# A hybrid S5/HGRN2 block: a hand-ordered front, S5 column work on GpSimd, and S5 input products stacked in 96 rows

## The chip, the cores and the metric

The kernel runs on one core of a Trainium2 chip. The metric is device time in microseconds of one execution; times are the median of several runs, and the profile is one further execution. The engines are TensorE (PE in the profile, with its weight loads as PEld), VectorE (DVE), ScalarE (ACT), GpSimd (POOL) and SyncE (SP, which only issues DMAs). Every engine works through its own instructions in order; semaphores tie the engines together.

## The reference

One decoder block on x of 256 tokens by 2048 channels in fp32, cut to what matters here:

```python
h = _rmsnorm(x, ln_mix_g[l])
proj = h @ w_in[l]                                # 2048 x 9216
u_s5, q_h, f_h, i_h, g_h, gate_s5, gate_hgrn = jnp.split(proj, _in_splits(), axis=-1)
y_s5 = _s5_branch(u_s5, ...) @ w_proj_s5[l]
y_hgrn = _hgrn2_branch(q_h, f_h, i_h, g_h, ...) @ w_proj_hgrn[l]
merged = jax.nn.sigmoid(gate_s5) * y_s5 + jax.nn.sigmoid(gate_hgrn) * y_hgrn
x = x + merged @ w_out[l]
x = x + _conv_glu_ffn(_rmsnorm(x, ln_ffn_g[l]), w_up[l], conv_w[l], conv_b[l], w_down[l])
return _rmsnorm(x, ln_final_g)

# inside _s5_branch: 64 groups of 16 channels, 64 states each
dt = jnp.exp(log_dt)[:, None]
mag = jnp.exp(lam_re * dt)
abar_re, abar_im = mag * jnp.cos(lam_im * dt), mag * jnp.sin(lam_im * dt)
coef_re, coef_im = ...                            # (abar - 1) / lambda, complex
bu_re = jnp.einsum('blgc,gpc->blgp', uf, b_re)    # and bu_im with b_im
bb_re, bb_im = ...                                # coef * bu, complex
...                                               # s[t] = abar * s[t-1] + bb[t]
y = einsum(s_re, c_re) - einsum(s_im, c_im) + d * uf
z = jax.nn.gelu(y)
z = z * jax.nn.sigmoid(z @ w_glu + b_glu)
```

## The kernel before

All large products run as **steps**. A step is 512 KB of weights (`[128, 1024]` fp32): `load_step` issues its load on SP's queue (tag `wr`, four buffers, issued LOAD_AHEAD = 5 steps ahead), `split_step` makes a high part `wh` (a cast on ACT, L256) and a low part `wl` (a subtraction on VectorE), two steps ahead (LA = 2, three buffers each), and TensorE adds up high x high, high x low and low x high. In `fm_job` (channels on partitions) a step is 8 matmuls of 512 columns on `wh` and 8 of 256 on `wl`; in `tm_job` (tokens on partitions) it is 12 of 512. There are 480 steps, executed in the order of their creation: 144 over w_in (u 16, q 16, g 16, f 16, the gates 64, v 16), 8 over w_glu, 16 and 16 over the two projections, 32 over w_out, 176 over w_up, 88 over w_down. Nearly every operation of VectorE and TensorE goes through the helper `Metered`, so these carry its line, L106, in the profile; tiles tell them apart.

**The front.** x (four chunks of 512 channels, 512 KB each) is loaded on SP between the first weights. `x_chunk(g)` transposes a chunk on TensorE into `ax` (PSUM), scales it by `g_mix` into the high part of `hT` on ACT (L405) and the low part on VectorE. `x_first` makes `g_mix` from `packG`, handles chunk 0 and puts dummy matmuls (`warm_up`) behind. The four u jobs come one after the other, four steps each (one for each chunk), so steps 0 to 3 need all four chunks; chunks 1 to 3 are transposed in the middle of steps 0 to 2 (`st.between`). `x_norm` (after step 2) adds the squares of x on VectorE and makes the row scale `r_x`, spread to `R_x` for the epilogues.

**Two side jobs** are Python generators. `side_run`, after every step, lets the current one advance while the planner's sum of VectorE costs is below that of TensorE, with at most two pauses (`yield`) a step for S5 and three for HGRN2; a yielded value means to wait until that job is finished. S5 comes first and must be done before the w_glu steps (index 144); HGRN2 follows and must be done at index 168. The rest of the order is left to the framework's compile-time scheduler, apart from places tied by `issue_after`.

`side_s5` loads b and c on ACT's queue (L585, L587), transposes parameters packed in rows (`packB`, `packC`) into columns, and then does about 130 small operations of 128x32 on VectorE: the HGRN2 lower bound, dt, the decay `mag_c`, the angle reduced in three parts (`hi`, `lo`), two sines on ACT (L663, L664), the input coefficients `cr` and `ci`. It builds tables of angles (`tabA`, `tabB`; summed for each ct on GpSimd by `angle_sum`, L741), the scaled b (`BB`) and the transposed c (`CT`). Then it loops over ct = 0 to 7 (128 channels each, two pairs). `b_trans(ct)` transposes two 128x128 blocks of b (`zmat`) and splits b and u into high and low parts in one tile; `b_proj(ct, pair)` multiplies them into the PSUM tile `bu`, twelve matmuls of 32 rows (3 parts, 2 components, 2 halves). VectorE rotates the result, runs four scans, rotates back, and TensorE applies c (`output`).

Parameters in rows come by small DMAs: eight on POOL's queue, four on SP's (`load_params`, behind the fifth weight load).

Of the kernel before, what the change touches and what calls it, by code (L numbers as in the profile page):

```python
# [17 lines left out]
P = 128  # L18
# [76 lines left out]
class Metered:  # L95
# [5 lines left out]
    def __getattr__(self, name):  # L101
        fn = getattr(self._e, name)

        def call(*args, **kw):
            self._load[self._key] += self._cost(name, args, kw)
            return fn(*args, **kw)  # L106
        return call
# [3 lines left out]
def kernel(  # L111
# [28 lines left out]
    WARM_H = 6  # L140
    NORM_AT = 2
# [35 lines left out]
    ones = cst.tile([P, P], F32, name="ones")  # L177
    G.memset(ones, 1.0)
# [7 lines left out]
    S.dma_start(out=cf, in_=cst_f)  # L186
    ident = cf[:, C_ID:C_ID + P]

    x_tok = [[unit() for _ in range(2)] for _ in range(2)]
# [8 lines left out]
    S.dma_start(out=packG, in_=rows(ln_mix_g))  # L198
    G.memset(packA, 0.0)
    ldt = pack[0:64, 5 * P:5 * P + 2]  # L200

    def load_params():
        S.dma_start(out=packA[16:32, :], in_=rows(lb_logits))
        S.dma_start(out=packA[56:72, :], in_=rows(ln_ffn_g))
        S.dma_start(out=packA[72:104, :], in_=a_re.rearrange("o (q g) p -> (o q) (g p)", g=2))
        S.dma_start(out=packB[0:32, :], in_=a_im.rearrange("o (q g) p -> (o q) (g p)", g=2))

# [8 lines left out]
    G.dma_start(out=packC[2][8:96, :], in_=rows(conv_b))  # L216
    masks = cst.tile([P, 5, 16], U8, name="masks")
# [22 lines left out]
    def weight_step(src, mm, need=None, extra_load=None):  # L240
        st = Step()
        st.src, st.mm, st.need, st.extra_load = src, mm, need, extra_load
        st.after = st.between = None
        steps.append(st)
        return st

    def load_step(st):
        uid[0] += 1
        st.w = wp.tile([P, 1024], F32, tag="wr", name=f"wr{uid[0]}", bufs=4)
        S.dma_start(out=v3(st.w, st.src.shape[1]), in_=st.src)  # L250

    def split_step(st):
# [3 lines left out]
        A.copy(st.wh, st.w)  # L256
# [14 lines left out]
    def fm_job(wap, c0, nkc, xs, epi, need=None, extra_load=None, wide=False):  # L271
# [5 lines left out]
        for g in range(ng):  # L277
            def mm(st, g=g):
                if g == 0:
                    box["ps"] = mm_bank()  # L280
                ps = box["ps"]
                wh, wl = v3(st.wh, 4), v3(st.wl, 4)
                for part in range(2):
                    if part == 1 and st.between is not None:
                        st.between()
# [107 lines left out]
    def x_chunk(g, between=None):  # L393

        for h in range(2):
            if h == 1 and between is not None:
                between()
# [5 lines left out]
            for a in range(2):  # L403
                kc = 4 * g + 2 * h + a
                A.activation(out=hT[:, kc, 0, :], in_=ax[:, a * T:(a + 1) * T], func=AF.Copy, scale=g_mix[:, kc:kc + 1])  # L405
# [5 lines left out]
        box["x"] = [getattr(i, "ins", i) for i in (last, lastp)]  # L411

    @contextmanager
    def behind_x():

        with tc.issue_after(box["x"][0]), tc.issue_after(box["x"][1]):
            yield

    def x_first():
        ax = axbank()  # L420
        PE.transpose(ax[:, 0:16], packG, ident[:16, :16])
        V.tensor_copy(g_mix, ax[:, 0:16])
        x_chunk(0, lambda: split_step(steps[0]))
        with behind_x():
            warm_up(WARM_H, ones)

    def x_norm():
        ss = cst.tile([P, 2, 4], F32, name="ss_x")
        for g in range(4):
            for j in range(2):  # L430
                xc = x_tok[j][g // 2][:, (g % 2) * 512:(g % 2) * 512 + 512]
                junk = tmp()
                V.scalar_tensor_tensor(out=junk, in0=xc, scalar=1.0, in1=xc, op0=ALU.mult, op1=ALU.mult,
                                       accum_out=ss[:, j, g:g + 1])
# [3 lines left out]
        broadcast_rows(R_x, r_x)  # L438
# [92 lines left out]
    u_jobs = [fm_job(w_in, 256 * p, 16, xs_hw, epi_u(p), wide=True) for p in range(4)]  # L531
# [25 lines left out]

    def exp_parts(new, xin):
# [18 lines left out]
        V.tensor_scalar(out=si, in0=n, scalar1=127.0, scalar2=8388608.0, op0=ALU.add, op1=ALU.mult)
        return e, si.bitcast(F32)

    def side_s5():  # L580

        bn, cn = unit(), unit()
        bn_r, bn_i = bn[:, 0:512], bn[:, 512:1024]
        for dst, src in ((bn_r, b_re), (bn_i, b_im)):
            A.dma_start(out=v3(dst, 32), in_=src.rearrange("o (q g) p c -> (o g p) q c", g=2))  # L585
        for dst, src in ((cn[:, 0:512], c_re), (cn[:, 512:1024], c_im)):
            A.dma_start(out=v3(dst, 8), in_=src.rearrange("o (t g) c p -> (o g c) t p", g=8))  # L587
# [14 lines left out]

        l0, l1 = colA[:, 16:24], colA[:, 24:32]
        m, e0, e1 = new()[:, 0:8], new()[:, 0:8], new()[:, 0:8]
        V.tensor_tensor(out=m, in0=l0, in1=l1, op=ALU.max)
        z = new()[:, 0:16]
        V.tensor_tensor(out=z[:, 0:8], in0=l0, in1=m, op=ALU.subtract)
        V.tensor_tensor(out=z[:, 8:16], in0=l1, in1=m, op=ALU.subtract)
        e, s = exp_parts(new, z)
        V.scalar_tensor_tensor(out=z, in0=e, scalar=1.0, in1=s, op0=ALU.add, op1=ALU.mult)  # L610
        V.tensor_tensor(out=e0, in0=z[:, 0:8], in1=z[:, 8:16], op=ALU.add)
        V.reciprocal(out=e1, in_=e0)
        V.tensor_tensor(out=lb_col, in0=z[:, 0:8], in1=e1, op=ALU.mult)
        V.tensor_scalar(out=oml_col, in0=lb_col, scalar1=-1.0, scalar2=1.0, op0=ALU.mult, op1=ALU.add)
        yield

        new = sp_tiles()
        lam_im = colB[:, 0:32]
        lam_re, dt_, la, th, mag, em1 = (new() for _ in range(6))
        V.tensor_scalar(out=lam_re, in0=colA[:, 72:104], scalar1=S5_MAX_RE, scalar2=None, op0=ALU.min)  # L620
        e, s = exp_parts(new, colB[:, 32:64])
        V.scalar_tensor_tensor(out=dt_, in0=e, scalar=1.0, in1=s, op0=ALU.add, op1=ALU.mult)
# [781 lines left out]
```

## Time and profile before

| | us |
|---|---|
| median of 3 runs | 1422.99 (1422.62 to 1424.28) |
| the profiled execution's own time | 1422.75 |
| its span | 1420.6 |
| TensorE busy | 1403.4 (99%) |
| VectorE busy | 1056.9 (74%) |
| ScalarE busy | 757.7 (53%) |
| GpSimd busy | 38.0 (3%) |
| read from HBM, written | 266.73 MB, 10.49 MB |

A row of the instruction view has start, length, engine, line, operation, tile written <- tiles read, shapes and how many are merged, then in brackets the idle time before it and what ended that. In groups the numbers after the bar are busy time in us and the mean in ns, then idle time before. The name `u` covers all the 4 KB work tiles, `t` the 2 KB ones, `d` scratch in DRAM. Ends of matmuls are modelled, so starts are the safer numbers for TensorE.

### The profile page before, as it was taken

The numbers are of one execution on the slowest core, as the hardware profiler recorded it, in microseconds if no ns is written. First come the engines' busy times: TensorE is split into PE (matmuls) and PEld (weight loads), VectorE is DVE, ScalarE is ACT, GpSimd is POOL, SyncE is SP. The second block draws the span as 40 slices with busy tenths as digits, with TensorE's granted clock in tenths as the row PEclk, the third lists the DMA queues.
The fourth block names the chain that finished last, engine by engine and source line by source line (L and its number), as shares of the span: only waits on it lengthen the run. The fifth ranks groups of instructions, "written<-read, shape, count | busy, mean of one in ns | idle before, by whom it ended". The sixth has DMA issues, their size and how long they took to land.

```text
span 1420.6 us, 20722 instructions
## 1 busy us (share of the span) xinstructions
PE 1403.4 (99%) x8008; PEld 1182.1 (83%) x8008; DVE 1056.9 (74%) x1453; ACT 757.7 (53%) x962; POOL 38.0 (3%) x33
## 2 busy tenths in 40 slices
PE   9999999999999999999999999999999999999997
PEld 7878887877778787888888888888888888888885
DVE  7999989998978968655777777777777775545454
ACT  5455576665655464454555555555555554434343
POOL 1040000000001000000000000000000000000000
PEclk9999999999999999999999999999999999999999
DMA  7865767666767466666666666666666666666653
GB/s 237 219 195 149 218 206 219 202 205 187 210 191 262 154 199 207 220 212 207 193 191 185 188 192 187 186 191 191 185 189 191 188 187 193 201 193 201 194 194 125
DMA packets 215940, 278.58 MB, mean 196 GB/s; under 512 B 19938, under 2 KB 141042, under 8 KB 215841
## 3 DMA queue, kind: packets, MB, share of 16 engines
q1 hardware_dynamic: 198496, 266.57, 60.5%
q10 hardware_dynamic: 17088, 10.49, 2.4%
q8 instruction: 63, 1.03, 0.3%
q14 instruction: 37, 0.30, 0.1%
q0 software_dynamic: 256, 0.19, 0.0%
HBM read 266.73 MB, written 10.49 MB: 195 GB/s over the span
## 4 chain that ended last, share of the span: by engine, by line
PE 95%; DVE 2%; DMA 1%; ACT 1%; issue 0%; POOL 0%; ACTq 0%; DVEq 0%; POOLq 0%
PE mm L106 87%; PE ax L106 7%; DVE u L106 1%; PE bu L106 1%; DMA u<-d 1%; DVE wl L106 1%; DMA u<-in_s_log_dt_dram 0%; ACT wh L256 0%; DVE t L106 0%; PE dummy L106 0%; DVE zmat L106 0%; ACT u L1275 0%; DVE x2g L106 0%; ACT hT L405 0%; ACT t L1259 0%
## 5 line engine op out<-in xcount | busy, mean ns | idle before, releaser
L256 ACT CAST wh<-wr 128x1024 fp32r<-128x1024 f32 x480 | 503.0, 1051 | 587.7 <-PE mm L106 424.2
L106 DVE TENSOR_TENSOR wl<-wr,wh 128x1024 fp32r<-128x1024 f32 x480 | 588.2, 1228 | 304.3 <-ACT wh L256 301.3
L106 PE MATMUL mm<-x2g,wh 128*128 128x512 f32 x1408 | 352.6, 392 | 0.0
L106 PEld LDWEIGHTS mm<-x2g,wh 128*128 128x128 f32 x1408 | 253.3, 189 | 45.3
L106 PE MATMUL mm<-wh,u 128*128 128x512 f32 x1040 | 260.7, 392 | 0.0
L106 PEld LDWEIGHTS mm<-wh,u 128*128 128x128 f32 x1040 | 193.7, 188 | 39.7
L106 PEld LDWEIGHTS mm<-x2g,wl 128*128 128x128 f32 x1408 | 192.0, 190 | 13.6
L106 PE MATMUL mm<-x2g,wl 128*128 128x256 f32 x1408 | 196.4, 282 | 0.0
L106 PE MATMUL mm<-wh,hT 128*128 128x512 f32 x768 | 193.6, 394 | 0.0
L106 PEld LDWEIGHTS mm<-wh,hT 128*128 128x128 f32 x768 | 142.1, 188 | 33.5 <-issue 2.9
L106 PE MATMUL mm<-wl,u 128*128 128x512 f32 x520 | 140.6, 390 | 0.0
L106 DVE TENSOR_TENSOR u<-u,u 128x512 f32<-128x512 f32 (+4 forms) x144 | 114.8, 821 | 0.5
L106 PEld LDWEIGHTS mm<-wl,u 128*128 128x128 f32 x520 | 97.4, 188 | 20.0
L106 PE MATMUL mm<-wl,hT 128*128 128x512 f32 x384 | 102.9, 390 | 0.0
L106 PE MATMUL mm<-hT,wh 128*128 128x512 f32 x384 | 100.4, 401 | 0.8 <-ACT wh L256 0.8
L106 PEld LDWEIGHTS mm<-wl,hT 128*128 128x128 f32 x384 | 72.1, 188 | 15.5
L106 PEld LDWEIGHTS mm<-hT,wh 128*128 128x128 f32 x384 | 69.9, 192 | 14.8 <-ACT wh L256 1.0
L106 DVE SCALAR_TENSOR_TENSOR t<-ub,colC,t 128x256 f32<-128x256 f32 x176 | 73.3, 479 | 0.0
L106 PEld LDWEIGHTS mm<-hT,wl 128*128 128x128 f32 x384 | 52.1, 191 | 4.7 <-DVE wl L106 1.3
L106 PE MATMUL mm<-hT,wl 128*128 128x256 f32 x384 | 54.3, 284 | 0.3 <-DVE wl L106 0.3
L1200 ACT ACTIVATE t<-ub,colC 128x256 f32<-128x256 f32 x88 | 48.0, 593 | 0.0
L106 PE MATMUL ax<-wh,u 128*128 128x512 f32 x176 | 43.3, 389 | 0.0
(186 smaller groups left out, 861.2 us busy)
## 6 DMA issues: line engine op xcount, KB each, us to landing
wr<-in_w_up_dram SPq DMA_DIRECT2D x176, 512.0 KB, 4.5
wr<-in_w_in_dram SPq DMA_DIRECT2D x144, 512.0 KB, 4.4
wr<-in_w_down_dram SPq DMA_DIRECT2D x88, 512.0 KB, 4.7
wr<-in_w_out_dram SPq DMA_DIRECT2D x32, 512.0 KB, 4.2
wr<-in_w_proj_s_dram SPq DMA_DIRECT2D x16, 512.0 KB, 4.0
wr<-in_w_proj_hgrn_dram SPq DMA_DIRECT2D x16, 512.0 KB, 4.8
d<-t ACTq DMA_DIRECT2D x28, 256.0 KB, 4.4
rl<-d SPq DMA_DIRECT2D x16, 256.0 KB, 4.3
```

The lines of the kernel that those rows point to most:

```text
L106: return fn(*args, **kw)
L256: A.copy(st.wh, st.w)
L1200: A.activation(out=av, in_=ub[:, a, 0:T], func=AF.Identity, scale=conv_col(0, n), bias=colC[:, 264 + n:265 + n])
```

## The change

1. **Order of the front.** The first twelve steps are re-sorted: for each chunk g of x, step g of the u jobs 0, 1 and 2 (FRONT = 3), so that a new chunk is needed every third step. The third job's PSUM bank is that of `bu`. x chunk g is loaded before step 3g's weights. Everything up to step 11 stands inside `manual_schedule` for SP, PE, ACT and DVE: their instructions keep the program's order. Weights are split one step ahead there, two afterwards.
2. **Start.** `packG` is loaded first, `cf` goes to ACT's queue, chunk 0 and step 0's weights come in halves (x on SP, weights on ACT's queue), `x_first` works by halves, step 0 runs by halves (`fine`: 24 matmuls of 256 columns), three dummies instead of six. `ones` is set on VectorE.
3. **Squares** of x move from VectorE to ACT (`x_squares`), one chunk at a time.
4. **Loads.** The four of `load_params` and the four of b and c move to POOL's queue, ahead of all other POOL work.
5. **S5 column work** moves from VectorE to GpSimd (`E = G`); a fused operation becomes two there (`fused`), so it is 126 operations, 82 of them ahead of the sines. Reciprocals and one maximum stay on VectorE. The side job starts after step 1; pauses ("step", n) hold it until step n: the sines wait for 12 and stand in ACT's order right behind the newest cast ("tied"), the reciprocals for 14 and 24. The lower bound comes after the coefficients.
6. **S5 input products.** `b_trans` splits b and u into two work tiles, writes each to DRAM and reads three parts back into 32-row bands (`stB`: high, high, low; `stU`: high, low, high), so that `b_proj` needs four matmuls of 96 rows in place of twelve of 32. `b_trans(ct+1)` moves from the middle of pair 0 to the head of tile ct, and six pauses follow `b_trans(0)` in place of one.

The core of the diff:

```diff
-    WARM_H = 6
-    NORM_AT = 2
+    WARM_H = 3
+    FRONT = 3
...
+    G.dma_start(out=packA[72:104, :], in_=a_re.rearrange("o (q g) p -> (o q) (g p)", g=2))
+    G.dma_start(out=packB[0:32, :], in_=a_im.rearrange("o (q g) p -> (o q) (g p)", g=2))
+    G.dma_start(out=packA[16:32, :], in_=rows(lb_logits))
+    G.dma_start(out=packA[56:72, :], in_=rows(ln_ffn_g))
...
+    bn, cn = unit(), unit()
+    for dst, src in ((bn[:, 0:512], b_re), (bn[:, 512:1024], b_im)):
+        G.dma_start(out=dst.rearrange("p (a b) -> p a b", a=32), in_=src.rearrange("o (q g) p c -> (o g p) q c", g=2))
+    for dst, src in ((cn[:, 0:512], c_re), (cn[:, 512:1024], c_im)):
+        G.dma_start(out=dst.rearrange("p (a b) -> p a b", a=8), in_=src.rearrange("o (t g) c p -> (o g c) t p", g=8))
...
+                if fine and g == 0:
+                    for h, part in ((0, 0), (0, 1), (0, 2), (1, 0), (1, 1), (1, 2)):
+                        for k in (2 * h, 2 * h + 1):
+                            for j in range(2):
+                                cols = slice(j * P, (j + 1) * P)
+                                o = ps[:, j, T:] if part == 1 else ps[:, j, :T]
+                                PE.matmul(o, (wl if part == 2 else wh)[:, k, cols], hT[:, k, part % 2, :],
+                                          start=k == 0 and part == 0, stop=False)
+                    return
...
+    def load_first():
+        st = steps[0]
+        st.w = wp.tile([P, 1024], F32, tag="wr", name=f"wr{uid[0]}", bufs=4)
+        for h in range(2):
+            for j in range(2):
+                S.dma_start(out=x_tok[j][0][:, h * T:(h + 1) * T], in_=x[0, j * P:(j + 1) * P, h * T:(h + 1) * T])
+            st.dma = A.dma_start(out=v3(st.w, 4)[:, 2 * h:2 * h + 2, :], in_=st.src[:, 2 * h:2 * h + 2, :])
...
+    def x_squares(g):
+        for j in range(2):
+            xc = x_tok[j][g // 2][:, (g % 2) * 512:(g % 2) * 512 + 512]
+            junk = tmp()
+            A.activation(out=junk, in_=xc, func=AF.Square, accum_out=ss_x[:, j, g:g + 1])
...
+    steps[:4 * FRONT] = [steps[4 * p + g] for g in range(4) for p in range(FRONT)]
...
+    E = G
+    def fused(out, in0, scalar, in1, op0, op1, t):
+        E.tensor_scalar(out=t, in0=in0, scalar1=scalar, scalar2=None, op0=op0)
+        E.tensor_tensor(out=out, in0=t, in1=in1, op=op1)
...
-        A.activation(out=sn, in_=pr, func=AF.Sin, scale=TWO_PI)
-        A.activation(out=sh, in_=pr, func=AF.Sin, scale=TWO_PI / 2)
+        yield ("step", 12)
+        with tc.issue_after(getattr(box["cast"], "ins", box["cast"])):
+            A.activation(out=sn, in_=pr, func=AF.Sin, scale=TWO_PI)
+            A.activation(out=sh, in_=pr, func=AF.Sin, scale=TWO_PI / 2)
...
+        yield ("step", 14)
+        with here():
+            V.reciprocal(out=den, in_=den)
...
-            c = bu_in[ct] = unit(F32R)
-            split_pair(c[:, 0:T], c[:, T:2 * T], ax[:, 0:2 * P])
-            split_pair(c[:, 2 * T:3 * T], c[:, 3 * T:4 * T], u_t.at(ct))
+            bc, uc = tmp(F32R), tmp(F32R)
+            split_pair(bc[:, 0:T], bc[:, T:2 * T], ax[:, 0:2 * P])
+            split_pair(uc[:, 0:T], uc[:, T:2 * T], u_t.at(ct))
+            for src, dst, parts in ((bc, stB, (0, 0, 1)), (uc, stU, (0, 1, 0))):
+                d = dram.tile([P, 512], F32R, name=f"st{uid[0]}")
+                G.dma_start(out=d, in_=src)
+                dv = d.rearrange("(q r) (s t) -> r s q t", q=4, s=2)
+                for j, part in enumerate(parts):
+                    G.dma_start(out=v3(dst[ct % 2], 4)[32 * j:32 * j + 32, :, :], in_=dv[:, part, :, :])
...
-            for i in range(2):
-                for j, (hb, hu) in enumerate(((0, 0), (0, 1), (1, 0))):
-                    for a in range(2):
-                        rows32 = slice(64 * pair + 32 * a, 64 * pair + 32 * a + 32)
-                        PE.matmul(bu[:, a, i * T:(i + 1) * T], c[rows32, hb * T + i * P:hb * T + (i + 1) * P],
-                                  c[rows32, (2 + hu) * T:(3 + hu) * T], start=j == 0, stop=j == 2)
+            sB, sU = v3(stB[ct % 2], 4), v3(stU[ct % 2], 4)
+            for a in range(2):
+                qq = 2 * pair + a
+                for i in range(2):
+                    PE.matmul(bu[:, a, i * T:(i + 1) * T], sB[0:96, qq, i * P:(i + 1) * P], sU[0:96, qq, :],
+                              start=True, stop=True)
...
         b_trans(0)
-        yield
+        for _ in range(6):
+            yield
...
+    with tc.manual_schedule(engines={ET.SP, ET.PE, ET.Activation, ET.DVE}):
+        load_first()
+        table_up()
+        for i in range(1, LOAD_AHEAD):
+            load_front(i)
+        warm_up(WARM, ones)
+        x_first()
+        for i in range(4 * FRONT):
+            g, r = divmod(i, FRONT)
+            load_front(i + LOAD_AHEAD)
+            if r == FRONT - 1 and g < 3:
+                x_chunk(g + 1)
+            split_step(steps[i + 1])
+            if i == 0:
+                x_squares(0)
+            elif r == FRONT - 1 and g < 3:
+                x_squares(g + 1)
+            work(i, steps[i])
+            if i == 3 * FRONT - 1:
+                x_norm()
+            elif i == 3 * FRONT + 1:
+                broadcast_rows(R_x, r_x)
+            if i == 1:
+                x_params()
+            if i >= 1:
+                pauses[0] = 0
+                load["dve"] = max(load["dve"], load["pe"] - 4.0)
+                side_run()
```

More of the change, by code (lines that the diff above doesn't have):

```diff
@@ L174, in at, with rows @@
             return self.units[k // 4][:, (k % 4) * T:(k % 4 + n) * T]
+    pack = unit()
+    packA, packB = pack[0:104, 0:P], pack[0:64, P:2 * P]
+    packC = [pack[0:P if i < 2 else 96, (2 + i) * P:(3 + i) * P] for i in range(3)]
+    def rows(ap):
+        return ap.rearrange("o (r c) -> (o r) c", c=P)
+    packG = pack[0:16, 6 * P:7 * P]
+    S.dma_start(out=packG, in_=rows(ln_mix_g))
     ones = cst.tile([P, P], F32, name="ones")
-    G.memset(ones, 1.0)
+    V.memset(ones, 1.0)
     epsc = cst.tile([P, 1], F32, name="epsc")
@@ L242, in weight_step @@
         st.src, st.mm, st.need, st.extra_load = src, mm, need, extra_load
-        st.after = st.between = None
+        st.after = None
         steps.append(st)
@@ L729, in side_s5 @@
             yield
+        yield ("step", 24)
+        with here():
+            V.reciprocal(out=e1, in_=e0)
+        E.tensor_tensor(out=lb_col, in0=z[:, 0:8], in1=e1, op=ALU.mult)
+        E.tensor_scalar(out=oml_col, in0=lb_col, scalar1=-1.0, scalar2=1.0, op0=ALU.mult, op1=ALU.add)
+        yield
         zmat = cst.tile([P, 2 * P], F32, name="zmat")
         G.memset(zmat, 0.0)
-        bu_in = {}
+        stB, stU = ([unit(F32R) for _ in range(2)] for _ in range(2))
         angles = {}
@@ L1326, in side_run, with load_front, work @@
                     return
-    for i in range(LOAD_AHEAD):
-        if i < 4:
-            load_x_chunk(i)
+    def load_front(i):
+        if i % FRONT == 0 and i < 4 * FRONT:
+            load_x_chunk(i // FRONT)
         load_step(steps[i])
-        if i == 4:
-            load_params()
-    table_up()
-    warm_up(WARM, ones)
-    x_first()
-    for i in range(1, LA):
-        split_step(steps[i])
-    for i in range(3):
-        steps[i].between = lambda i=i: x_chunk(i + 1)
-    load["dve"] = load["pe"] = 0.0
-    for i, st in enumerate(steps):
-        if i + LOAD_AHEAD < len(steps):
-            load_step(steps[i + LOAD_AHEAD])
-        if i + LA < len(steps):
-            split_step(steps[i + LA])
+    def work(i, st):
         run_later(i=i)
@@ L1356 @@
             st.extra_load()
+        fin.add(("step", i))
         st.mm(st)
[L1358 to L1361 removed]
         if st.after is not None:
             job, fn = st.after
[L1364 to L1372 removed]
+            later.append((i + (2 if i < 4 * FRONT else 1), job, fn))
+    ET = mybir.EngineType
+    with tc.manual_schedule(engines={ET.SP, ET.PE, ET.Activation, ET.DVE}):
+        load["dve"] = load["pe"] = 0.0
+        load_first()
[25 more added lines that the diff above has]
+                side_run()
+    for i in range(1, LA):
+        split_step(steps[4 * FRONT + i])
+    for i, st in enumerate(steps):
+        if i < 4 * FRONT:
+            continue
+        if i + LOAD_AHEAD < len(steps):
+            load_front(i + LOAD_AHEAD)
+        if i + LA < len(steps):
+            split_step(steps[i + LA])
+        work(i, st)
+        load["dve"] = max(load["dve"], load["pe"] - 4.0)
+        pauses[0] = 0
+        side_run()
     run_later(i=len(steps) + 10)
```

256 lines of the change are left out of this document (122 added, 134 removed).

## The prediction

> **What bounds the kernel now.** I read the page first, then a table of stretches, then the first 113 us instruction by instruction.
>
> ```profile
> span 1420.6 us, 20722 instructions
> PE 1403.4 (99%) x8008; PEld 1182.1 (83%) x8008; DVE 1056.9 (74%) x1453; ACT 757.7 (53%) x962; POOL 38.0 (3%) x33
> PE 95%; DVE 2%; DMA 1%; ACT 1%; issue 0%; POOL 0%; ACTq 0%; DVEq 0%; POOLq 0%
> ```
>
> TensorE carries 95% of the chain that ended last, so an edit pays only if it shortens TensorE's work or closes a gap in it. Its 99% hides gaps, since ends of matmuls are modelled; I therefore count finished steps against the clock. In the table of stretches the columns are PE, PEld, DVE, ACT, POOL, clock, DMA share, GB/s:
>
> ```profile
> 10.56:49.97 39.41, 38.57 (x227) 32.89 (x226) 35.16 (x109) 19.86 (x29) 0.00 (x0) 1.00 0.83 232
> 49.97:112.68 62.71, 60.11 (x342) 52.15 (x340) 58.06 (x129) 34.20 (x43) 14.70 (x4) 0.97 0.64 197
> 112.68:448.87 336.19, 336.04 (x1743) 271.20 (x1743) 310.27 (x369) 201.79 (x227) 11.96 (x6) 1.00 0.66 200
> ```
>
> From 112.68 to 448.87 TensorE has no gap. Before that VectorE is full (58.06 of 62.71 us) and TensorE is not. The price of a step is read from TensorE's instructions in order of time (start, length, operation, idle before):
>
> ```profile
> 10.56 2.08 PE L106 MATMUL mm<-hT,wh 128*128 128x512 f32 x8
> ...
> 47.07 2.12 PE L106 MATMUL mm<-hT,wh 128*128 128x512 f32 x8 [0.78 <-ACT wh L256]
> ...
> 49.97 2.00 PE L106 MATMUL mm<-hT,wh 128*128 128x512 f32 x8
> 51.81 1.12 PE L106 MATMUL mm<-hT,wl 128*128 128x256 f32 x8
> 52.77 2.00 PE L106 MATMUL mm<-hT,wh 128*128 128x512 f32 x8
> ...
> 91.35 1.21 PE L106 MATMUL mm<-hT,wl 128*128 128x256 f32 x8 [0.27 <-DVE wl L106]
> ...
> 101.50 1.14 PE L106 MATMUL ax<-cf,u 128*128 128x128 f32 x8 [2.33 <-DVE u L106]
> 102.32 3.67 PE L106 MATMUL mm<-hT,wh 128*128 128x512 f32 x8
> 105.82 1.12 PE L106 MATMUL mm<-hT,wl 128*128 128x256 f32 x8
> ...
> 112.68 0.98 PE L106 MATMUL bu<-u 32*128 32x256 f32 x12
> 113.58 2.11 PE L106 MATMUL mm<-wh,hT 128*128 128x512 f32 x8
> ```
>
> One step of 16 matmuls takes 52.77 - 49.97 = 2.80 us; eight transposes take 102.32 - 101.50 = 0.82, so 0.10 each; a 256-column matmul takes (52.77 - 51.81)/8 = 0.12. After the gap of 2.33 us the next eight matmuls need 3.50 instead of 1.84 us, 1.7 more, with the mean clock of that stretch at 0.97. The groups of the stretch up to 112.6 give the amount done:
>
> ```profile
> L106 PE MATMUL mm<-hT,wh 128*128 128x512 f32 x256 | 67.9, 404 | 0.8 <-ACT wh L256 0.8
> L106 PE MATMUL ax<-cf,u 128*128 128x128 f32 x50 | 9.0, 301 | 3.7 <-DVE u L106 2.3 <-DMA u<-in_x_dram 1.1 <-DVE g_mix L106 0.3
> ```
>
> 256 / 8 = 32 steps precede the first S5 product: 89.6 us of work, and some 60 transposes and small products (6.0). About 17 us of the first 112.68 are something else: the start, and waits for VectorE.
>
> **The front, up to step 12.** The start now waits for a whole chunk of x, and g_mix waits on VectorE behind a copy that waits for a POOL load:
>
> ```profile
> 5.67 0.48 PE L106 MATMUL ax<-cf,u 128*128 128x128 f32 x1 [1.10 <-DMA u<-in_x_dram]
> 5.70 0.45 DVE L106 COPY u<-u 32x128 f32<-32x128 f32 x1 [3.27 <-DMA u<-in_s_log_dt_dram]
> 6.18 0.17 DVE L106 COPY g_mix<-ax 128x16 f32<-128x16 f32 x1
> 8.05 2.45 PEld L106 LDWEIGHTS dummy<-ones 128*128 128x128 f32 x12
> ```
>
> The change takes that copy out of g_mix's way, loads the first x chunk in halves, brings step 0's weights on ACT's queue beside them and halves the dummies (twelve records in 2.45 us: six are 1.2). I let the second half of x land at 5.7, where the whole chunk lands now; 8 transposes (0.8) and the dummies (1.2) put the first matmul at about 7.6, not 10.56. Step 0 as 24 products of 256 columns is 24 x 0.12 = 2.9, as before. Three steps per x chunk give 8.4 us of work between chunks, so transposes no longer starve it: 7.6 + 12 x 2.80 + 24 chunk transposes (2.4) + nine small ones (0.9) = 44.5. Now step 12 starts at 49.97: **-5.5**.
>
> **Steps 12 to 31.** Ideal 20 x 2.80 + 18 x 0.10 = 57.8, now 62.7: **-4.9** if VectorE no longer holds TensorE. It loses eight squares and the column work:
>
> ```profile
> L106 DVE SCALAR_TENSOR_TENSOR t<-u 128x512 f32<-128x512 f32 x8 | 5.0, 680 | 0.0
> L106 DVE TENSOR_TENSOR wl<-wr,wh 128x1024 fp32r<-128x1024 f32 x480 | 588.2, 1228 | 304.3 <-ACT wh L256 301.3
> L448 ACT COPY t<-mm 128x512 f32<-128x512 f32 x7 | 4.1, 585 | 0.2 <-PE mm L106 0.2
> ```
>
> The split itself, 1.23 us a step of 2.80, stays, so VectorE keeps over half of each step free. The squares go to ACT, some 8 x 0.59 by the copy of that size; ACT is busy 19.86 of 39.41 us, so they are hidden. What is late next is the cast wh on ACT, as in the 0.78 above.
>
> Of the moved loads: on SP the later x chunks now stand behind weights that wait for a buffer. Chunk 2 is behind step 5's weights, whose buffer comes free with step 1's split at about 10 us, and is wanted at about 23 (7.6 + 5 x 2.80 + 1.3): covered. The b and c loads move from ACT's queue at 37 us to POOL's at 8 us, beside those weights; by the same 12 us of lead I take 0 (up to 4, if a chunk is late all the same). The four loads that leave SP join POOL's, so conv_b becomes the twelfth there:
>
> ```profile
> u<-in_conv_b_dram POOLq DMA_DIRECT2D x1, 44.0 KB, 5.4
> L214 POOL DMA_DIRECT2D u<-in_conv_w_dram x1 | 0.5, 549 | 0.0
> ```
>
> Issued at 1.4 + 11 x 0.55 = 7.4, it lands at 12.8 (5.4 us, last column); its transpose stands in TensorE's fixed order behind step 1, which ends at 13.2. Covered by 0.4 us; uncovered it costs what it is late. The masks' load, now behind step 12's weights, is wanted at 448 only.
>
> As remainder I leave two waits of the kind that stays, 0.78 + 0.27, **+1.0**. Front: -9.4, between -3.0 (only the earlier start) and -10.4.
>
> **S5 products.** Twelve 32-row matmuls take 113.58 - 112.68 = 0.90. Four 96-row ones of 256 columns are not in the trace; I price them like the 128-row ones, 4 x 0.12 = 0.48. 16 x 0.42 = **-6.7**; the ends are 0 (VectorE, 310.27 of 336.19 us busy, could set the pace) and -9.6 (each as short as a 32-row one now, 0.90/12 = 0.075).
>
> **The bounce through DRAM.** Each b_trans adds two writes of 256 KB and six reads on POOL's queue, and a wait there: reads queue behind the landing of their write. Behind them on POOL are only the next angle_sum and the column work, both earlier in time. The nearest rows (KB, us from issue to landing) and, from the chain of waits, two products that follow each other:
>
> ```profile
> d<-t ACTq DMA_DIRECT2D x28, 256.0 KB, 4.4
> rl<-d SPq DMA_DIRECT2D x16, 256.0 KB, 4.3
> ...
> 116.74 0.98 PE bu L106 x12
> 134.53 0.91 PE bu L106 x12
> ```
>
> A write and a read are 4.4 + 4.3, with issues (1.1 for both writes, 1.6 for three reads) and splits (0.8) some 12 us; with the two tiles strictly one after the other 19. For ct 0 the six pauses, at two a step, cover 3 x 2.80 = 8.4. So TensorE waits 3.6 to 10.6 once, or 0 if the compiled order puts the product later. I take the near end, 3.6, as both writes can go out together, with the 1.7 that followed the 2.33 gap: **+5.3**, range 0 to 12.3. Later tiles have more: products (0,1) and (1,0) alone stand 134.53 - 116.74 = 17.8 us apart, and b_trans(1) now precedes both and the half tile before. The traffic, 8 x 1.25 MB in 336 us, is small beside a DMA share of 0.66. The Trainium skill (DMA: Bandwidth & Descriptors, "Anatomy of one DMA - SWDGE (gpsimd) path") prices one such DMA at 2.0 us plus bytes by 436 GB/s, an estimate of 2.6 us for 256 KB; by it the bounce is covered and the term is 0. The trace's 4.4 and 4.3 speak against it.
>
> **Sum.** The profiled execution took 1422.75 us (span 1420.6 and 2.15 around it; median of the runs 1422.99). 1422.75 - 9.4 - 6.7 + 5.3 = 1411.95, say **1412**. What follows 448.87 is the same work; S5 ends near step 144 in both and is paced by the meters, whose TensorE load falls by only 16 x 0.22 = 3.5 us. At 0 to 2 us I leave that out.
>
> **Rivals.** *Late sines (slower).* The sines wait on ACT for 82 dependent POOL operations of 128x32, and behind them in ACT's queue stand the casts, on which TensorE lives. POOL's and ACT's rows:
>
> ```profile
> 77.83 11.68 POOL L741 TENSOR_TENSOR u<-u 128x1024 f32<-128x1024 f32 x3 [71.63 <-DVE u L106]
> 184.60 1.94 POOL L741 TENSOR_TENSOR u<-u 128x1024 f32<-128x1024 f32 x1 [36.39 <-DVE u L106]
> 0.24 0.10 POOL L1389 MEMSET const-float32-0.0<- 128x1 f32 x1 [0.24 <-issue]
> 37.70 4.24 ACTq L585 DMA_DIRECT2D u<-in_s_b_im_dram  x1
> 41.97 3.19 ACTq L587 DMA_DIRECT2D u<-in_s_c_re_dram  x1
> L106 DVE TENSOR_SCALAR t<-u 128x512 f32<-128x512 f32 x2 | 0.8, 418 | 0.0
> 83.48 4.25 DVE L106 TENSOR_SCALAR u<-u,cf 128x512 f32<-128x512 f32 x2
> 95.32 5.24 DVE L106 TENSOR_TENSOR wl<-wr,wh 128x1024 fp32r<-128x1024 f32 x3 [0.59 <-ACT wh L256]
> ```
>
> 0.10 at one column and 1.94 at 1024 give 0.16 at 32. The same addition took 3.9 beside a full VectorE, and VectorE's two scalings 4.25 us where two of that size took 0.8 elsewhere: the two engines hold each other up. With wl running 40% of the time I take 0.16/0.6 = 0.26. POOL is free of loads at about 16.4: twelve issues to 7.9, then four large ones, which I let block it as long as they blocked ACT's queue (37.70 to 45.16, 7.5, and two of 0.5). The sines' input is then ready at 16.4 + 82 x 0.26 = 38. TensorE stalls only past about 51.8: step 12 starts at 44.5, casts for two more steps are out (8.4), and the next needs 1.1. The point is (51.8 - 16.4)/82 = 0.43 per operation. If each meets a running split of 1.2 half way, 0.16 + 0.6 = 0.76, the input comes at 79: 27 us late, **1439**. Against it: VectorE has gaps in the new front. Chance 0.17. The Trainium skill (SBUF - State Buffer, "Who interferes with whom") has a VectorE operation with two SBUF inputs and a GpSimd read exclude each other for a whole instruction; wl is one, and the rows at 77.83 and 95.32 agree.
>
> *The bounce is covered* (short legs, or the product ordered later): 1422.75 - 9.4 - 6.7 = **1406.7**. 0.20.
>
> *The S5 saving doesn't arrive*, VectorE at 92% setting the pace: 1422.75 - 9.4 + 5.3 = **1418.7**; the same if the split waits on POOL and only the start is won (1422.75 - 3.0 - 6.7 + 5.3 = 1418.4). 0.14.
>
> *It cancels*: bounce at 12.3 and half the front, 1422.75 - 4.7 - 6.7 + 12.3 = **1423.7**. 0.07.
>
> **Chances.** Forecast 0.42. A measurement of this kernel can tell about 0.2% (2.85 us) from no change. Faster: 0.42 + 0.20 + 0.12 of the 0.14 = 0.74; same 0.02 + 0.06 = 0.08; slower 0.17 + 0.01 = 0.18. The range 1404 to 1425 leaves out the late sines and little else.
>
> **What would show it.** Right: first mm near 7.6; twelve steps done by 45; the first bu near 103 plus a gap of 4 to 5 us on TensorE before it, with matmuls at half pace behind; bu x64 in groups of 0.48; no gap at the later bu. Wrong: ACT idle before the Sin with POOL as releaser; POOL's 128x32 operations spaced over 0.43 us; gaps before every bu; wl over 1.3 us through the front.

## The result, and the profile after

The changed kernel takes **1430.5 us** (median of four runs, 1428.82 to 1432.21) beside 1422.87 for the kernel before on the same chip (four runs, 1422.62 to 1424.28): 1.0052 times as long, 95% interval 1.0040 to 1.0065. It is slower by half a per cent; 1412 and "faster" were forecast. The profiled execution took 1432.21 us, the longest of the four.

The head of the page, and the chain that ended last:

```profile
span 1430.4 us, 20608 instructions
PE 1398.9 (98%) x7882; PEld 1180.4 (83%) x7882; DVE 1042.4 (73%) x1327; ACT 763.4 (53%) x980; POOL 131.3 (9%) x230
PE 84%; DVE 4%; POOL 4%; DMA 3%; issue 2%; ACT 1%; SPq 0%; ACTq 0%; DVEq 0%; POOLq 0%
```

TensorE is busy 4.5 us less than before and still ends later: its share of the chain falls from 95% to 84%, and DVE, POOL and DMA take what it gave up. The table of stretches shows where. Its columns are length, then busy time of PE, PEld, DVE, ACT and POOL, the granted clock, DMA share and GB/s. The cuts are the first matmul, step 12, the end of 32 steps, the first w_glu matmul and the first w_up matmul:

```profile
8.67:48.08 39.41, 38.66 (x235) 34.39 (x235) 25.47 (x45) 24.34 (x45) 33.58 (x82) 1.00 0.84 250
48.08:106.69 58.61, 58.44 (x343) 51.29 (x341) 48.62 (x74) 34.07 (x45) 37.99 (x63) 1.00 0.67 202
106.69:451.60 344.91, 330.99 (x1614) 267.57 (x1612) 315.32 (x365) 201.70 (x227) 47.19 (x65) 0.99 0.78 225
451.60:688.22 236.62, 231.12 (x1788) 189.35 (x1785) 159.08 (x221) 119.41 (x188) 5.62 (x2) 0.99 0.63 203
```

The last of these stretches in the kernel before, which the prediction did not show:

```profile
448.87:678.25 229.38, 227.78 (x1785) 186.71 (x1784) 159.40 (x220) 118.06 (x188) 5.89 (x2) 1.00 0.65 209
```

The front works: 32 steps are done at 106.69 instead of 112.68 (-6.0). The S5 stretch gives that back: 344.9 instead of 336.2 (+8.7). The stretch from w_glu to w_up, of which the change alters no instruction, takes 236.6 instead of 229.4 (+7.2). Together +9.97, which is the difference between the first w_up matmuls (688.22 and 678.25).

In the S5 stretch TensorE is idle for 13.9 us (344.91 - 330.99; before, 0.15): 7.42 at the first bounce, shown next, and 6.5 in small waits further on, two thirds of them for the high and low parts of the weights. These small waits take up nearly all of the 6.7 us that the cheaper products were to save.

The first bounce, on POOL's queue (start, time spent on issuing, operation, idle before) and then on TensorE:

```profile
98.54 1.23 POOL L835 DMA_DIRECT2D st<-t  x2 [5.66 <-DVE t L106]
103.11 1.65 POOL L838 DMA_DIRECT2D u<-st  x3 [3.34 <-DMA st<-t]
105.48 1.62 POOL L838 DMA_DIRECT2D u<-st  x3 [0.72 <-DMA st<-t]
```

```profile
92.27 0.38 PE L106 MATMUL ax<-cf,zmat 128*128 128x128 f32 x2
...
106.69 2.00 PE L106 MATMUL mm<-wh,hT 128*128 128x512 f32 x8
108.53 0.61 PE L106 MATMUL mm<-wl,hT 128*128 128x512 f32 x2
116.57 1.19 PE L106 MATMUL bu<-u,u 96*128 96x256 f32 x4 [7.42 <-DMA u<-st]
...
118.41 2.63 PE L106 MATMUL mm<-wh,hT 128*128 128x512 f32 x8
120.88 1.07 PE L106 MATMUL mm<-wl,hT 128*128 128x512 f32 x4
```

The transposes of tile 0 (`ax<-cf,zmat`) stand at 92.27; the splits behind them on ACT and VectorE are done only 6.3 us later, at 98.54. There the two writes go out together, and POOL's waits for them end at 103.11 and 105.48. The reads are all issued by 107.1, but TensorE gets its data only at 116.57, 18.0 us after the first write and 24.3 after the transposes. In between it works on other steps until 109.15 and then waits. From 106.69 to 118.41 TensorE does a step (2.7 us) and a product (0.5), so 8.5 us are lost; the next eight matmuls still take 2.47 instead of 1.81, which makes some 9.2. The groups of DMA issues (KB, median us from issue to landing):

```profile
u<-st POOLq DMA_DIRECT2D x48, 128.0 KB, 6.0
st<-t POOLq DMA_DIRECT2D x16, 256.0 KB, 5.5
```

The end of HGRN2 on TensorE in the changed kernel:

```profile
538.80 1.98 PE L106 MATMUL mm<-wh,u 128*128 128x512 f32 x8
540.61 1.07 PE L106 MATMUL mm<-wl,u 128*128 128x512 f32 x4
544.30 1.55 PE L106 MATMUL ax<-cf,u 128*128 128x128 f32 x6 [2.62 <-DVE u L106]
...
548.92 2.48 PE L106 MATMUL mm<-wh,u 128*128 128x512 f32 x5
551.20 1.48 PE L106 MATMUL mm<-wl,u 128*128 128x512 f32 x3
```

TensorE waits 2.62 us for VectorE's scaling of HGRN2's outputs and then works at half pace: five 512-column matmuls take 2.28 us (548.92 to 551.20), where eight took 1.81 ahead of the wait (538.80 to 540.61). The table of stretches has a granted clock of 0.50 there:

```profile
546.50:553.00 6.50, 6.16 (x18) 4.48 (x18) 4.32 (x13) 2.73 (x5) 0.00 (x0) 0.50 0.23 69
```

### The profile page after: what moved, and what is told of

It reads as the page before. It is cut to its first block, busy times and chain, and to the rows that moved or that the text cites. A ratio compares the mean times of both kernels' runs of the same rounds, so it can differ in the third digit from the quotient of the medians.

```text
span 1430.4 us, 20608 instructions
## 1 busy us (share of the span) xinstructions
PE 1398.9 (98%) x7882; PEld 1180.4 (83%) x7882; DVE 1042.4 (73%) x1327; ACT 763.4 (53%) x980; POOL 131.3 (9%) x230
## 4 chain that ended last, share of the span: by engine, by line
PE 84%; DVE 4%; POOL 4%; DMA 3%; issue 2%; ACT 1%; SPq 0%; ACTq 0%; DVEq 0%; POOLq 0%
PE mm L106 77%; PE ax L106 7%; DVE u L106 2%; DVE wl L106 2%; DMA wr<-in_w_in_dram 1%; DMA u<-st 1%; PE bu L106 1%; DMA wr<-in_w_proj_s_dram 1%; ACT wh L260 0%; POOL u L634 0%; POOL u L633 0%; DMA st<-t 0%; POOL u L617 0%; DMA t<-d 0%; POOL u L616 0%
## 5 line engine op out<-in xcount | busy, mean ns | idle before, releaser
L106 DVE TENSOR_TENSOR wl<-wr,wh 128x1024 fp32r<-128x1024 f32 (+1 forms) x481 | 592.9, 1236 | 321.9 <-ACT wh L260 309.6
L106 DVE TENSOR_TENSOR u<-u,u 128x512 f32<-128x512 f32 (+2 forms) x132 | 107.4, 840 | 0.5
L106 PE MATMUL mm<-hT,wh 128*128 128x512 f32 (+1 forms) x360 | 89.7, 392 | 0.0
L106 PEld LDWEIGHTS mm<-hT,wh 128*128 128x128 f32 x360 | 64.7, 192 | 11.2
L106 PEld LDWEIGHTS mm<-hT,wl 128*128 128x128 f32 x352 | 48.1, 191 | 3.5 <-DVE wl L106 0.2
L106 PE MATMUL mm<-hT,wl 128*128 128x256 f32 x352 | 49.3, 282 | 0.0
```

Source lines behind the costliest of these rows:

```text
L106: self.last = fn(*args, **kw)
```

## The experiments

All comparisons are medians against the kernel before on the same chip (1422.87 for the change; 1422.71 for experiments 1 to 4, 1423.13 for the others, 17 to 26 runs of it each). The last column is from the one profiled execution of each kernel; those of 1 (1421.68), 4 (1423.19), 6 (1424.59) and 8 (1418.47) lie 2 to 4 us off their medians.

| kernel | median us | ratio to before, 95% | w_glu to w_up |
|---|---|---|---|
| the change | 1430.50 | 1.0052 [1.0040, 1.0065] | 236.6 |
| 1 front alone | 1424.03 | 1.0005 [0.9996, 1.0014] | 228.0 |
| 2 late order | 1418.86 | 0.9971 [0.9960, 0.9982] | 229.8 |
| 3 traffic | 1418.69 | 0.9972 [0.9962, 0.9982] | 228.8 |
| 4 products | 1421.35 | 0.9990 [0.9981, 0.9999] | 235.9 |
| 5 products, meter | 1415.94 | 0.9954 [0.9942, 0.9966] | 229.2 |
| 6 the change, meter | 1427.65 | 1.0036 [1.0023, 1.0049] | 230.5 |
| 7 tile 0 direct | 1419.99 | 0.9978 [0.9969, 0.9986] | 235.5 |
| 8 tile 0 direct, meter | 1414.92 | 0.9948 [0.9933, 0.9963] | 232.3 |
| 9 slow meter | 1424.20 | 1.0000 [0.9991, 1.0010] | 235.7 |
| 10 one pause | 1421.59 | 0.9985 [0.9976, 0.9994] | 228.4 |
| 11 tile 0 direct, meter, four pauses | 1413.50 | 0.9929 [0.9917, 0.9941] | 228.4 |

**1. The front alone.** Part 6 of the change is undone.

```diff
-            bc, uc = tmp(F32R), tmp(F32R)
+            c = bu_in[ct] = unit(F32R)
...
-        for _ in range(6):
-            yield
+        yield
```

> The change with its S5 part wholly undone: the old twelve 32-row products, the old place of b_trans in the middle of a tile, one pause, no transfers through DRAM. Theory A (the bounce through DRAM is the whole loss, by its wait, its traffic, and S5 ending later): only the 6.0 us that the new front showed remain, 1422.9 - 6.0 = 1416.9 (1415 to 1418.5), w_glu starts near 443 and the stretch from there to w_up takes 238.7 as before. Theory B (the new front or the column work on GpSimd shifts S5 against the fixed steps, so that HGRN2 is squeezed whatever the bounce does): 1422 to 1425, with 245 to 246 us from w_glu to w_up.

Measured: 1424.03, within Theory B's numbers, but not for its reason: from w_glu to w_up it takes 228.0 us, not 245. (The 245 of the expectation was read from a later mark, at which the kernel before has 238.7; in the table's terms Theory B expected 236.) TensorE loses time at the first product:

```profile
97.98 0.50 PE L106 MATMUL bu<-u 32*128 32x256 f32 x4 [1.51 <-ACT u L264]
100.89 1.14 PE L106 MATMUL bu<-u 32*128 32x256 f32 x8 [2.42 <-DVE u L106]
101.97 3.24 PE L106 MATMUL mm<-hT,wh 128*128 128x512 f32 x8
```

With one pause the product stands right behind the transposes, and TensorE waits for the split of b and u on ACT and VectorE, then does eight matmuls in 3.07 us (to 105.04) instead of 1.84: 5.2 us in all. In this kernel the new front brings nothing; how much of that is due to the waits, experiment 10 asks. Both theories fall.

**2. The late order.** As 1, with the change's six pauses and b_trans at the head of a tile.

```diff
-        yield
+        for _ in range(6):
+            yield
         bu = b_proj(0, 0)
...
+            if ct < 7:
+                b_place(ct + 1)
+                yield u_jobs[(ct + 1) // 2]
+                b_trans(ct + 1)
+                yield
             for pair in range(2):
```

> As the front alone, but with the change's six pauses before the first product and b_trans moved to the head of a tile; old products, no transfers. It prices the order alone. Theory A1 (S5 ends later because of the pauses, and squeezes HGRN2): some 7 us over the front alone, near 1424, S5's last output beyond 448 us less the front's gain, and 245 us from w_glu to w_up. Theory A2 (order costs nothing, only the transfers do): within 1 us of the front alone, near 1417.

Measured: 1418.86, in neither theory's place relative to 1 (5.2 us under it), but at A2's own figure of "near 1417" within 2 us. The order costs nothing; it gains. The first two products:

```profile
101.00 0.98 PE L106 MATMUL bu<-u 32*128 32x256 f32 x12
...
110.00 0.98 PE L106 MATMUL bu<-u 32*128 32x256 f32 x12 [0.63 <-DVE u L106]
```

The first comes without a gap.

**3. The traffic.** As 2, with the change's DMAs into tiles that nothing reads.

```diff
+            for src, dst, parts in ((c[:, 0:512], stB, (0, 0, 1)), (c[:, 512:1024], stU, (0, 1, 0))):
+                d = dram.tile([P, 512], F32R, name=f"st{uid[0]}")
+                G.dma_start(out=d, in_=src)
...
```

> As the late order, with the old products, and the change's eight transfers a tile issued on GpSimd's queue into tiles that nothing reads: the traffic without the wait. Theory T (traffic delays the weight loads and so the S5 stretch): 5 to 7 us over the late order, with loads of in_w_in of 15 us and more on the chain. Theory W (the first wait of 7.4 us and the slow clock behind it carry the loss): within 2 us of the late order.

Measured: 1418.69 beside 1418.86. The traffic alone costs nothing that can be measured, which is theory W's number. What the first wait costs is not tested here but in experiment 7.

**4. The products.** The change without its DMAs: the products read a copy of `BB`, so the real operands are left out of them.

```diff
-        stB, stU = ([unit(F32R) for _ in range(2)] for _ in range(2))
+        st1 = unit(F32R)
+        A.copy(st1, BB)
+        stB, stU = [st1, st1], [st1, st1]
...
-            for src, dst, parts in ((bc, stB, (0, 0, 1)), (uc, stU, (0, 1, 0))):
...
```

> The change without its transfers: the products of 96 rows read one tile of other data, so the bounce is left out of the computation; order and pauses as in the change. If the saving of 16 x 0.42 us reaches the end: 6.7 us under the late order (1417.5 if that is 1424, 1410.5 if it is 1417). If VectorE or the meters pace S5, it is within 1.5 us of the late order.

Measured: 1421.35, 2.5 us *over* the late order, though TensorE has less to do and nothing waits for DRAM. Neither expectation holds. The 236 us from w_glu to w_up are here again, so they come neither from the bounce nor from the pauses. What is left is that the products are cheaper, which experiments 5 and 9 test. `side_run` hands out S5 and HGRN2 while the summed price of VectorE's work is below that of TensorE's. Twelve 32-row matmuls stand in that sum at 12 x 0.0545 = 0.654 us, four 96-row ones at 4 x 0.109 = 0.436. Counted in the order in which the programs are generated (no time is in it):

```
                                     S5 ended at     HGRN2 ended at   parts still left at step 144, 168
before; 2, 3, 5, 6, 8                step 144        step 167         0, 0
the change; 4, 7, 9                  step 144        step 168         4, 2
11                                   step 143        step 166         0, 0
1, 10                                step 141        step 164         0, 0
```

At steps 144 and 168 what is left is put into the engines' queues in one go, ahead of that step's matmuls.

**5, 6. The meter.** One line, which gives the planner's sum for TensorE (its meter) the price of the old products again, added to 4 and to the change:

```diff
             bu = psb.tile([P, 2, 512], F32, tag="bu", name=f"bu{uid[0]}")
             uid[0] += 1
+            load["pe"] += 0.218
```

> As the products without transfers (the bounce is left out, the 96-row products read other data), with one thing more: each product pair adds 0.218 to TensorE's meter, the difference between the meter's price of twelve 32-row and of four 96-row matmuls, so that S5 is given out over the same steps as with the old products. Theory F (the cheaper price in the meter slows S5 by some steps, its last parts and those of HGRN2 are forced out in one go at steps 144 and 168, and TensorE waits there): the saving arrives, 1418.9 - 6.7 = 1412 (1410.5 to 1414), and from w_glu to w_up 229 to 230 us instead of 235.9. Theory V (VectorE paces S5, and whatever TensorE saves turns into waits for wl): within 1.5 us of the late order, 1417.5 to 1420.5, with the lost time between 110 and 445 us.

> The change with the same addition of 0.218 per product pair to TensorE's meter, and nothing else. Theory F: 6 to 7 us less than the change, 1424, with 229 to 230 us from w_glu to w_up instead of 236.6. Theory V: the 6 us move from HGRN2 into S5 as waits for wl, total within 2 us of 1430.5.

Measured: 1415.94 for 5, 5.4 us under 4; from w_glu to w_up 229.2 us:

```profile
442.44:671.66 229.22, 227.69 (x1786) 186.57 (x1784) 159.44 (x220) 118.18 (x188) 6.20 (x2) 1.00 0.65 209
```

Theory F holds for that stretch, but the total misses its 1412, and part of theory V is in it. Against the late order only 2.9 of 6.7 us arrive. From the end of 32 steps to w_glu TensorE is idle for 5.7 us in 5 (333.01 with 327.27 busy) and for 1.2 in the late order (335.72 with 334.48 busy). The longest wait of 5 is here (TensorE, then VectorE in the same stretch):

```profile
185.23 2.00 PE L106 MATMUL mm<-hT,wh 128*128 128x512 f32 x8
190.25 1.21 PE L106 MATMUL mm<-hT,wl 128*128 128x256 f32 x8 [3.03 <-DVE wl L106]
191.30 3.33 PE L106 MATMUL mm<-hT,wh 128*128 128x512 f32 x8
194.43 1.39 PE L106 MATMUL mm<-hT,wl 128*128 128x256 f32 x8
```

```profile
182.92 1.21 DVE L106 TENSOR_TENSOR wl<-wr,wh 128x1024 fp32r<-128x1024 f32 x1
184.05 1.28 DVE L106 TENSOR_TENSOR u<-u,u 128x512 f32<-128x512 f32 x2
185.37 2.44 DVE L106 TENSOR_TENSOR_SCAN u<-mag,u 128x256 f32<-128x256 f32 x4
187.84 1.22 DVE L106 TENSOR_TENSOR u<-u,u 128x1024 f32<-128x1024 f32 x1
188.98 2.35 DVE L106 TENSOR_TENSOR wl<-wr,wh 128x1024 fp32r<-128x1024 f32 x2
```

Between two splits VectorE has 4.9 us of S5 (184.05 to 188.98), and a step lasts 2.8. VectorE is the limit here, and the wait with its slow clock costs 4.3 us (3.03, and 3.13 instead of 1.84 for the eight matmuls from 191.30 to 194.43). For 6: 1427.65, 2.9 us less than the change, short of the 6 to 7 expected, though its stretch of 230.5 is what theory F has. Its profiled execution is the fastest of its five, that of the change the slowest of its four, so the traces overstate what the line is worth there.

**7, 8. Tile 0 without the bounce**, alone and with the meter's line for tiles 1 to 7:

```diff
-            bc, uc = tmp(F32R), tmp(F32R)
+            bc, uc = (stB[0][:, 0:512], stU[0][:, 0:512]) if ct == 0 else (tmp(F32R), tmp(F32R))
...
+            if ct == 0:
+                c, cu = stB[0], stU[0]
...
+                return bu
```

> The change, but tile 0's products are the old twelve matmuls straight from the split, without the bounce; tiles 1 to 7 bounce as in the change. If only the first bounce is exposed: the wait of 7.42 us and the slow clock behind it go, two products cost 0.42 each more, 1430.5 - 8.1 + 0.8 = 1423 (1422 to 1424.5); w_glu to w_up stays at 236. If each bounce is late (tile 1 becomes the first exposed one): within 3 us of the change.

> Tile 0 without the bounce and the meter's addition together (for tiles 1 to 7). If the two losses add: 1430.5 - 7.3 - 6.5 = 1416.7, and 1413 (the late order less 14 x 0.42) if the small waits in S5 go as well, which would be below the kernel before by 0.4 to 0.7%. If VectorE paces S5: 1418.5 to 1421.

Measured: 1419.99 for 7, 10.5 us less than the change, more than the 7.3 expected; the stretch from w_glu to w_up stays at 235.5, as foreseen. No later product waits for a DMA. For 8: 1414.92, another 5.1 us less, between the two figures expected if the losses add, and 0.5% below the kernel before. Its profiled execution, at 1418.47, lies at the slow end of its spread; the stretch is 232.3 there.

**9. The slow meter.** As 2, with no instruction changed:

```diff
+            load["pe"] -= 0.218
             c = bu_in[ct]
```

> The late order (old products, no transfers; 1418.9) with 0.218 taken off TensorE's meter per product pair: no instruction changes, only the steps over which S5 and HGRN2 are given out, as the cheaper products set them. Theory F (the price in the meter alone makes the late end): 5 to 6 us more, 1424 to 1425, w_glu to w_up 235 to 236 us instead of 229.8. Theory V (what was lost came from cheaper TensorE work itself): within 1.5 us of 1418.9.

Measured: 1424.20, 5.3 us over the late order, and 235.7 from w_glu to w_up. The wait of the changed kernel is back at the same place:

```profile
532.86 1.07 PE L106 MATMUL mm<-wl,u 128*128 128x512 f32 x4
536.55 1.71 PE L106 MATMUL ax<-cf,u 128*128 128x128 f32 x6 [2.62 <-DVE u L106]
```

This settles theory F: 16 times 0.218 us in the planner's sum cost 5.3 us of time, with the same work. (That is its price in the late order; in the change itself experiment 6 has 2.9.)

**10. One pause** in the late order, to part the two differences between 1 and 2:

```diff
-        for _ in range(6):
-            yield
+        yield
         bu = b_proj(0, 0)
```

> The late order with one pause instead of six before the first product. It parts the two things in which the front alone (1424.0) and the late order (1418.9) differ. If the pauses bring the gain (they cover the split between the transposes and the first product, where the front alone waited 1.51 and 2.42 us with a slow clock behind): 1423 to 1425. If b_trans at the head of a tile brings it: 1418 to 1420.

Measured: 1421.59, between the two expectations. The gaps of 1 are back:

```profile
98.58 0.50 PE L106 MATMUL bu<-u 32*128 32x256 f32 x4 [1.51 <-ACT u L264]
101.50 1.22 PE L106 MATMUL bu<-u 32*128 32x256 f32 x8 [2.42 <-DVE u L106]
```

So the five further pauses bring 2.7 us and the place of b_trans 2.4; why the place brings that much was not found. The 2.7 are a balance: with one pause S5 ends three steps earlier (table in 4), and the stretch from w_glu to w_up is 1.4 us shorter.

**11. Four pauses** in kernel 8.

```diff
-        for _ in range(6):
+        for _ in range(4):
```

> Tile 0 without the bounce and the meter's addition together (1414.9), with four pauses instead of six: S5 and HGRN2 end one step earlier. If the small waits that are left come from S5's lateness: 1 to 2 us less, 1413 to 1414. If the pauses only cover the first split, four still do: 1414 to 1416. If four are too few for it: 1417 to 1420, with a gap ahead of the first bu.

Measured: **1413.50**, 0.9929 of the kernel before [0.9917, 0.9941] and 17 us below the change: the fastest of all. Its page's engines and chain, and its last stretch:

```profile
PE 1393.6 (99%) x7898; PEld 1178.5 (83%) x7898; DVE 1036.9 (73%) x1327; ACT 763.0 (54%) x979; POOL 129.1 (9%) x222
PE 91%; DVE 5%; ACT 1%; issue 1%; DMA 0%; SPq 0%; ACTq 0%; DVEq 0%
```

```profile
441.08:669.46 228.38, 227.35 (x1786) 187.00 (x1785) 157.78 (x219) 117.47 (x186) 5.38 (x2) 1.00 0.64 209
```

DMA has left the chain, and S5 and HGRN2 end a step earlier than with six pauses. Its 1.4 us on kernel 8 lie inside the spread of 8's runs (1412.28 to 1418.98).

The stacked products on the old front were not tried, so that the front is worth the same with and without them is assumed, not shown.

## Why the prediction was wrong

The sum foresaw -10.8 us and +7.6 were measured, 18.4 us apart. The runs divide this into four differences along the chain before, 2, 5, 4, the change:

| term | forecast | measured | off by |
|---|---|---|---|
| front, with the late order | -9.4 | 1418.86 - 1422.71 = -3.9 | 5.5 |
| cheaper products | -6.7 | 1415.94 - 1418.86 = -2.9 | 3.8 |
| late end of S5 and HGRN2 | left out | 1421.35 - 1415.94 = +5.4 | 5.4 |
| bounce | +5.3 | 1430.50 - 1421.35 = +9.2 | 3.9 |

(The kernel before differs by up to 0.4 us between these sets of runs; that is left in. The four add up to 18.6.) The shares depend on the path: on the changed kernel itself the late end is worth 2.9 us (experiment 6), and leaving out the first bounce 10.5 (experiment 7).

**What bounds the kernel.** Right: each loss that the traces locate is a gap on TensorE or matmuls at half pace.

**The front, up to step 12: -5.5, got -1.9.** The mechanism is right, the start was mis-sized. From the changed kernel, and below it from experiment 6, which has the same front:

```profile
8.67 2.02 PE L106 MATMUL mm<-hT,wh 128*128 128x256 f32 x8
...
12.44 2.00 PE L106 MATMUL mm<-hT,wh 128*128 128x512 f32 x8
...
15.23 0.25 PE L106 MATMUL ax<-cf,u 104*128 104x104 f32 x1
16.14 1.97 PE L106 MATMUL ax<-cf,u 64*128 64x64 f32 x12 [0.65 <-PE ax L106]
17.86 2.09 PE L106 MATMUL mf<-hT,wh 128*128 128x512 f32 x8
```

```profile
8.09 1.20 PE L106 MATMUL mm<-hT,wh 128*128 128x256 f32 x8
9.12 0.64 PE L106 MATMUL mm<-hT,wl 128*128 128x256 f32 x4
```

The first matmul comes at 8.67, not 7.6 (1.1 us). Step 0 takes 3.77, not 2.9, its first eight matmuls 1.85 instead of 0.96: they run at half pace (0.9). The halved dummies alone don't explain it: in experiment 6, with the same instructions up to there, the eight took 1.03 (8.09 to 9.12); in experiment 9 they took 1.85 again, with a granted clock of 0.50 from 8.2 to 11.5 us. What decides between the two is open. Among the twelve profiles with this front the first matmul comes between 8.09 and 9.95. The parameter transposes with the eight of chunk 1 take 2.63 (15.23 to 17.86) where the sum had 0.8 + 0.5 (1.3).

In the trace of the change the whole front falls 3.4 us short (6.0 of 9.4); where the rest of the table's 5.5 goes is open.

**Steps 12 to 31: -4.9, with +1.0 for waits.** Right: 58.6 us, -4.1. What the step left out is the product behind them. With its old single pause the front alone gains nothing (experiment 1).

**S5 products: 16 x 0.42.** The price is right (232.80 to 233.27 in the changed kernel is 0.47 for one). That it reaches the end is where the rival *the S5 saving doesn't arrive* was partly right: 2.9 of 6.7 us. In experiment 5 the rest stands as idle time of TensorE (5.7 us instead of 1.2 up to w_glu), with VectorE as the limit in places, as at 185 us; the changed kernel has 6.5 us of it beside the bounce.

**The bounce: +5.3.** The mechanism is right: one wait at the first product and a slow clock behind it. Both sides of the subtraction were mis-sized. The way from the splits to the data was priced at some 12 us, with 0.8 for the splits and 4.4 + 4.3 for a write and a read. It took 24.3 from the transposes on: 6.3 until the splits were done and 18.0 from the first write, of which POOL's waits for the two writes ended after 4.6 and 6.9, and the six reads took 7.7 to 9.9 each from issue to landing. The cover was put at the pauses' 8.4; it was 16.9 (92.27 to 109.15), because the compiled order put the product some 8 us later, which the prediction had as a possibility that would make the term 0. In experiment 2 the old product stands 8.7 us behind the transposes (92.33 to 101.00). The two errors partly cancel: 7.42 us of wait instead of 3.6. The Trainium skill (DMA: Bandwidth & Descriptors, "Anatomy of one DMA - SWDGE (gpsimd) path"), by whose formula a write of 256 KB takes an estimated 2.6 us, is contradicted by the median of 5.5 for these writes. "Later tiles have more" and "the traffic is small" both held: no later product waits for a DMA, and experiment 3 finds no cost.

**"What follows 448.87 is the same work ... At 0 to 2 us I leave that out".** This is the step whose mechanism failed; the three above were terms of the wrong size. The prediction had the number in hand: the meter's TensorE load falls by 3.5 us. It took that for 0 to 2 us of delay. But in the kernel before S5 ends at step 144, which demands it, and HGRN2 at 167, one ahead of its own. There was no room: with 3.5 us less in the sum four parts of S5 and two of HGRN2 are left over. Issued in one go, they make TensorE wait at 541 us for VectorE's chain, and the clock falls behind the gap. Experiment 9 prices this at 5.3 us with no instruction changed; the traces have 7.2 us in the change (against the kernel before) and 6.1 in experiment 4 (against the late order). In the change itself the one line of experiment 6 brought back only 2.9; how much of the 7.2 the late end makes there is open.

**Late sines.** Did not happen, but by less than the sum said. From the changed kernel, POOL's operations beside VectorE's splits, and ACT's wait:

```profile
17.02 0.23 POOL L712 TENSOR_TENSOR u<-u 128x32 f32<-128x32 f32 x1
...
47.80 1.14 POOL L669 TENSOR_TENSOR u<-u 128x32 f32<-128x32 f32 x1
49.58 1.30 POOL L695 TENSOR_SCALAR u<-u 128x32 f32<-128x32 f32 x1
```

```profile
47.56 1.28 DVE L106 TENSOR_TENSOR wl<-wr,wh 128x1024 fp32r<-128x1024 f32 x1
...
49.41 1.27 DVE L106 TENSOR_TENSOR wl<-wr,wh 128x1024 fp32r<-128x1024 f32 x1
```

```profile
54.10 0.23 ACT L705 ACTIVATE u<-u 128x32 f32<-128x32 f32 x1 [4.42 <-POOL u L701]
```

Operations of one size took 0.23 us outside the splits and 1.14 and 1.30 when they began inside one, ending 0.1 and 0.2 us after it (48.94 and 50.88, the splits 48.84 and 50.68). The rule of the Trainium skill (SBUF - State Buffer, "Who interferes with whom") agrees with these rows. From 15.89 to 54.08, 82 operations took 0.47 us each, not 0.26, and over the deciding point of 0.43. Two of the four signs named as "wrong" were there, ACT idle before the sine and POOL's spacing, and TensorE still had no gap: step 12 started 3.6 us later than forecast, which moves the point of stalling from 51.8 to 55.4, and the input came at 54.1. It held with 1.3 us to spare, not 14. That is luck: against the forecast's own point of 51.8 the input was 2.3 us late, and only the late front made room.

**The other rivals.** *The bounce is covered* is nearest to experiment 7, where nothing waits for a bounce, but at 1420.0, not 1406.7. *It cancels* had the bounce dear and half the front gone, which is what happened to those two terms; it lacked the late end and kept the whole S5 saving.

## What to carry to other kernels

A planner that hands out side work by estimated costs is part of the schedule: making an operation cheaper on the engine that it counts can push the side work past its deadline, so after such an edit ask what is left over at each forced step, not only what the edit saves. A bounce through DRAM should be priced from the operation that makes its data (here the transposes) to landing of the last read under the load of that moment, and the first use, which has no earlier tile to hide behind, treated by itself; here the old products for one tile of eight brought back 10 us. And a gain at the front of a kernel counts only up to the next wait: look at what that wait depends on before adding it up.

## What the runs showed of the hardware

- Reads of 128 KB into 32 partitions took as long from issue to landing as writes of twice the size from 128 partitions, or longer: medians of 6.0 us (2.6 to 9.9) and 5.5 (2.3 to 11.2) in the changed kernel, 5.0 and 5.0 in experiment 6.
- A gap of 2.6 us on TensorE cost more than itself: in the changed kernel the granted clock behind it was 0.50 from 546.5 to 553 us, and the stretch lost 7.2 us in all. A gap need not have this effect: in experiment 6 TensorE waited 3.26 us for a cast (until 194.84), and the granted clock from 195 to 205 us was 1.00.
